# A two-layer hybrid block: operands ahead of a stage border, another order of seven products, and one pass over the context rows

## The chip, the core and the metric

The kernel runs on one core of one Trainium2 chip. The metric is device time in microseconds (us) of one execution. The core has five engines that run side by side, each with its own queue of instructions: TensorE (PE in the profile, its weight loads are PEld), VectorE (DVE), ScalarE (ACT), GpSimd (POOL) and SyncE (SP, which issues nearly all transfers here). TensorE adds up its results in PSUM banks; everything else lives in SBUF tiles.

## The reference

Two layers over 1024 latent tokens and 256 context tokens of width 1024. Each layer mixes tokens (attention, a Fourier transform, a gated mixing), projects, and then runs a squared-ReLU MLP whose result goes through a gate into the residual. The second layer (`last`) updates the latent tokens alone.

```python
def squared_relu_mlp(h, w1, w2):
    return jnp.square(jax.nn.relu(h @ w1)) @ w2

def layer(x, ctx, c, c_ctx, ..., w_out, w1, w2, update_ctx):
    ...
    x = x + gt1 * mix_x
    x = x + gt2 * squared_relu_mlp(modulate(rms_norm(x, g2), sh2, sc2), w1, w2)
    if update_ctx:
        ...
        ctx = ctx + cgt2 * squared_relu_mlp(modulate(rms_norm(ctx, g2), csh2, csc2), w1, w2)
    return x, ctx
```

`w1` is 1024 x 4096, `w2` is 4096 x 1024, all in 32-bit floats.

## The kernel before

**Precision.** Each matrix product is made of three matmuls on operands split into a high and a low part: high x high, high x low, low x high (`mm3`, lines 194 to 196). A split is a cast on ACT (the high part) and a subtraction on DVE (the low part).

**Tokens** come in quads: quad 0 and quad 1 are 512 latent tokens each, quad 2 the 256 context tokens (first layer only).

**First MLP stage** (from line 1641). The 4096 hidden columns are 32 groups of 128, taken in the order p, p+16. For each group and quad, `hidden` makes 24 matmuls, then a ReLU on ACT and a product on DVE into a T tile. After each pair of groups `combine` (line 1485) forms seven left operands from the four hidden tiles of quads 0 and 1 and stores them to DRAM (`tdram[1]` to `tdram[7]`): two as they are, three sums on DVE and two on POOL (line 1494). The context's hidden tiles are stored apart (`put_ctx`, `cdram`).

**Second MLP stage for the latent tokens** (from line 1681). The product with `w2` is done as seven products of half-size blocks instead of eight (Strassen's scheme, `prods`). `turns` is their order. Each product runs over 16 chunks, an item each: `fetch` loads the chunk's left operand (R tiles, two chunks a load) and its block rows of `w2` (blocks 11 and 22 stay in S tiles, with four in L tiles, once loaded; 12 and 21 are loaded into W2 tiles for each use), four items ahead; `split` casts and subtracts the left operand (T tiles, lines 1566 and 1567), sums two weight blocks on POOL where the product needs it (an M tile, line 1573), and splits the sum (W1 tiles, lines 1575 and 1577), two items ahead; `product` makes 4 x 3 matmuls of 512 columns into four PSUM banks. When a product is through, `take` calls wait in the list `todo` and are issued one or two per item: in the first layer they add the gated bank to the residual, in the last to the output tile `z` (its first write is a copy on ACT, line 1613, the others an addition on DVE, line 1615). In the last layer `settle` (line 1617) finishes an output half tile: load of the residual, two POOL operations (lines 1624 and 1625) and, where it is complete, the store. Products 3 and 4 need no sum of weights, the other five need 16 sums each.

The contributions fix when an output block is complete: block (1,1) takes products 4, 1, 5, 7; (2,1) takes 4, 2; (1,2) takes 3, 5; (2,2) takes 3, 1, 2, 6. In the first layer quad 0 is block column 1, and `finish_quad(0)`, the next layer's norm of quad 0 (square sums on ACT and POOL, scaling on DVE, ACT and POOL), starts when it is complete.

**Second MLP stage for the context** (from line 1724, first layer only). The output's 1024 columns are two halves; for each half all 32 chunks are run: `split_ctx` loads 128 rows of `w2`, half the columns (an R tile), and the chunk of context rows (an M tile), and splits both (W1 and T tiles, lines 1730 to 1736), two steps ahead; then 4 x 3 matmuls of 256 columns go into four banks. So the context rows are loaded and split twice.

**What sets the order.** Instructions are written in the order of the program text, but each engine's queue is made by a scheduler that can issue a later instruction earlier when its buffer and operands are there. Tiles of one tag share a fixed number of buffers, and `allocate_in_order` forces them to be taken in program order:

```python
NBUF = {"S": 40, "L": 12, "T": 8, "M": 4, "R": 3, "W1": 8, "W2": 8, "pB": 5}
```

At the border of the two stages the program text has: the last group's hidden tiles (with the loads of items 0 and 1 after its first quad), the last `combine`, the loads of items 2 and 3, then `split(0)` and `split(1)`.

Of the kernel before, what the change touches and what calls it, by code (L numbers as in the profile page):

```python
# [11 lines left out]
F32 = mybir.dt.float32  # L12
# [6 lines left out]
P = 128  # L19
D = 1024  # L20
KC = D // P
# [106 lines left out]
def hybrid_block_kernel(ctx: ExitStack, tc: tile.TileContext, a: dict, out: bass.AP):  # L128
# [45 lines left out]
    def load(dst, src):  # L174
        nc.sync.dma_start(dst, src)
# [420 lines left out]
    def layer(l, ys, norms, bank):  # L596
# [923 lines left out]
        if not last:  # L1520
# [8 lines left out]
                 3: ((11,), None, ((1, 2, 1), (2, 2, 1))), 4: ((22,), None, ((1, 1, 1), (2, 1, 1))),  # L1529
                 5: ((11, 12), ALU.add, ((1, 1, -1), (1, 2, 1))), 6: ((21, 11), ALU.subtract, ((2, 2, 1),)),  # L1530
                 7: ((12, 22), ALU.subtract, ((1, 1, 1),))}
        turns = (4, 3, 1, 5, 7, 2, 6)
        items = [(i, c) for i in turns for c in range(NP)]
        ares, anow, traw, parts_of = {}, {}, {}, {}

# [14 lines left out]
        def fetch(n):  # L1550
            i, c = items[n]
            if c % 2 == 0:
                traw[i, c] = R(2, 512)
                load(flat(traw[i, c]), tdram[i][:, c * 512:(c + 2) * 512])
            for b in prods[i][0]:
                if b in (11, 22):
                    if (b, c) not in ares:
                        ares[b, c] = a_load(b, c)
                else:
                    anow[b, c] = a_load(b, c)  # L1560
# [43 lines left out]
        def take(o, i, j, b, sign):  # L1604
            if not last:
                x, k = xm[j - 1], 4 * (i - 1) + b
                gate = mods[l, 5][:, 0, k:k + 1] if sign > 0 else ngate[:, k:k + 1]
                V.scalar_tensor_tensor(x.chunk(k), o, gate, x.chunk(k), ALU.mult, ALU.add)
                return
            t = out_tile(i, j, b)  # L1610
            if (i, j, b) not in seen:
                seen.add((i, j, b))
                A.copy(t, o)
            else:
                V.tensor_tensor(t, t, o, ALU.add if sign > 0 else ALU.subtract)

# [24 lines left out]
        for n in range(2, NFF):  # L1641
            c = order[n]
            w1c = w1n
            if n + 1 < NFF:
                w1n = split_rows(w1d, order[n + 1], "W1")
            for qi in range(len(quads)):
                hq[c, qi] = hidden(w1c, qi)
                if qi < 2:
                    pump(1)
                if n == NFF - 1 and qi == 0:  # L1650
                    fetch(0)
                    fetch(1)
            if not last:
                put_ctx(c)
            if n % 2:
                combine(c - NP)
        for n in (2, 3):
            fetch(n)
        split(0)
        split(1)  # L1660


        todo = []
# [17 lines left out]
        for n, (i, c) in enumerate(items):  # L1681
            if n + 4 < len(items):
                fetch(n + 4)
            if n + 2 < len(items):
                split(n + 2)
            if c == 0:
                banks = [PB(512) for _ in range(4)]
            tail = last and i == turns[-1]
            if tail and c >= NP - 3:
                if c < NP - 1:  # L1690
                    continue
                assert not todo
                for b in range(4):
                    for cc in range(NP - 3, NP):
                        product(n - NP + 1 + cc, b, banks[b])
                    end_row(banks[b], b)
                continue
            for b in range(4):
                product(n, b, banks[b])
            parts_of.pop(n)  # L1700
            if c > 1 or todo:
                for _ in range(1 if len(todo) < 8 else 2):
                    if todo:
                        todo.pop(0)()
            if side is not None and not todo:
                step(side, 2)
            pump(1)
            if c == NP - 1:
                for b in range(4):
                    for ti, tj, sign in prods[i][2]:  # L1710
                        todo.append(lambda o=banks[b], ti=ti, tj=tj, b=b, sign=sign: take(o, ti, tj, b, sign))
                if last:
                    ready = {5: ((1, 2, True),), 7: ((1, 1, True),), 2: ((2, 1, True), (2, 2, False))}.get(i, ())
                    for b in range(4):
                        for ti, tj, done in ready:
                            todo.append(lambda ti=ti, tj=tj, b=b, done=done: settle(ti, tj, b, done))
                elif i == 2:
                    side = finish_quad(0)
        while todo and last:
            todo.pop(0)()  # L1720
        if not last:
            finish_bg()

            x = xm[2]

            def split_ctx(c, half):
                raw = alloc("R", [512], F32)
                load(raw, w2d[c * P:(c + 1) * P, half * 512:(half + 1) * 512])
                sh, sl = alloc("W1", [512], F32R), alloc("W1", [512], F32R)
                A.copy(sh, raw)  # L1730
                V.tensor_sub(sl, raw, sh)  # L1731
                m = M(256)
                load(m, cdram[:, c * 256:(c + 1) * 256])
                th, tl = pair(T, 256)
                A.copy(th, m)  # L1735
                V.tensor_sub(tl, m, th)  # L1736
                return th, tl, sh, sl

            citems = [(half, c) for half in range(2) for c in range(NFF)]
            ahead = [split_ctx(c, half) for half, c in citems[:2]]  # L1740
            wk, wk_gen = [], None
            for n, (half, c) in enumerate(citems):
                if n + 2 < len(citems):
                    ahead.append(split_ctx(citems[n + 2][1], citems[n + 2][0]))
                if c == 0:
                    banks = [PB(512) for _ in range(4)]
                th, tl, sh, sl = ahead.pop(0)
                for b in range(4):
                    f = slice(b * P, (b + 1) * P)
                    mm3(banks[b][:, 0:256], sh[:, f], sl[:, f], th, tl, c == 0, c == NFF - 1)  # L1750
                if todo:
                    todo.pop(0)()
                elif next(side, 0) == 0 and 1 not in nsum:
                    side = finish_quad(1)
                if half == 1 and c >= 16 and len(wk) < 4 and c % 4 == 0:
                    if wk_gen is None:
                        wk_gen = split_cols(k_pair(("W2", "W1")), a["w_in"][l + 1], 512, 512, L)
                    wk.append(next(wk_gen))
                if c == NFF - 1:
                    for b in range(4):  # L1760
                        k = 4 * half + b
                        V.scalar_tensor_tensor(x.chunk(k), banks[b][:, 0:256], mods[l, 5][:, 1, k:k + 1], x.chunk(k),
                                               ALU.mult, ALU.add)
            run(side)
            run(finish_quad(2))
            return ny, nnorm, (wk, wk_gen)
# [36 lines left out]
```

## Time and profile before

| | |
|---|---|
| median of 3 runs | 2804.55 us (2801.64 to 2808.71) |
| profiled execution | 2804.51 us |
| its span, first to last instruction | 2802.7 us |
| TensorE busy | 2693.4 us, 96% |
| DVE, ACT, POOL busy | 1852.9, 1314.7, 802.4 us |
| mean granted TensorE clock | 0.989 |
| mean DMA rate | 143 GB/s |

Busy time of TensorE overlaps from matmul to matmul, so a busy share of 96% is no measure of its speed; the number of matmuls in a stretch is. A row of the waits or of the timeline names in brackets how long an engine stood idle before an instruction, and what ended that idle time. In the profiled execution the first layer's seven products end at about 1476.7 us and its context pass at about 1592.4; the second layer's products run from 2474.3 to the end.

### The profile page before, as it was taken

Reading aid. Unit: us, or ns where it says so; the run is one execution under the profiler, and the core shown is the slowest. Engines: PE = TensorE matmul, PEld = TensorE weight load, DVE = VectorE, ACT = ScalarE, POOL = GpSimd, SP = SyncE. Lnnn points to the kernel's source line nnn. Section 1 sums busy time; section 2 is a strip of 40 time slices with the busy share of each in tenths; the row PEclk is TensorE's granted clock in tenths of the full one; section 3 lists DMA queues with packets and bytes.
Section 4 is the critical chain, followed back from the end, with each engine's and each line's share of the span. In section 5 each row is a group of like instructions: output and inputs, shape, how many; then the busy total and the mean of one; then the engine's idle time right before and its main releaser. Section 6 shows DMA issues by size and latency. Waiting matters only on the chain.

```text
span 2802.7 us, 39268 instructions
## 1 busy us (share of the span) xinstructions
PE 2693.4 (96%) x13620; PEld 2216.3 (79%) x13620; DVE 1852.9 (66%) x3461; ACT 1314.7 (47%) x2885; POOL 802.4 (29%) x650
## 2 busy tenths in 40 slices
PE   7899898999999999999998999999999999999998
PEld 5677687887888888788878887788888888878876
DVE  7787979767766555465567674888774333354697
ACT  6536878665211111244446534888753222235432
POOL 4221755411011010104451001533211111112587
PEclk9999999999999999999999999999999999999999
DMA  8435221424445454635747723132235333383563
GB/s 281 137 117 153 75 87 47 126 73 158 139 149 182 147 171 149 222 121 166 240 136 219 225 76 121 59 93 70 84 122 190 132 124 128 124 270 98 184 227 115
DMA packets 310919, 401.91 MB, mean 143 GB/s; under 512 B 23336, under 2 KB 201920, under 8 KB 310720
## 3 DMA queue, kind: packets, MB, share of 16 engines
q1 hardware_dynamic: 305568, 390.23, 43.0%
q0 software_dynamic: 5152, 9.18, 1.2%
q8 instruction: 107, 1.75, 0.3%
q14 instruction: 92, 0.75, 0.1%
HBM read 297.87 MB, written 101.45 MB: 142 GB/s over the span
## 4 chain that ended last, share of the span: by engine, by line
PE 63%; DMA 3%; DVE 3%; issue 2%; POOL 2%; ACT 2%; SPq 0%; ACTq 0%; DVEq 0%; POOLq 0%
PE pB L194 19%; PE pB L195 19%; PE pB L196 19%; DMA R<-in_w_mlp 2%; PE pB L1118 2%; PE pB L1131 1%; PE pB L1132 1%; DVE W L1577 1%; PE pB L1039 1%; PE pB L1040 1%; ACT W L1730 0%; DVE T L1567 0%; ACT L L1101 0%; POOL L L1624 0%; PE pB L336 0%
## 5 line engine op out<-in xcount | busy, mean ns | idle before, releaser
L194 PE MATMUL pB<-S,W 128*128 128x512 f32 (+1 forms) x1600 | 599.0, 375 | 2.2 <-ACT S L470 1.6
L196 PE MATMUL pB<-S,W 128*128 128x512 f32 (+1 forms) x1600 | 596.2, 373 | 1.4 <-DVE W L591 1.4
L195 PE MATMUL pB<-S,W 128*128 128x512 f32 (+1 forms) x1600 | 595.4, 373 | 0.3 <-DVE S L475 0.3
L194 PEld LDWEIGHTS pB<-S,W 128*128 128x128 f32 x1600 | 300.7, 188 | 60.3 <-ACT S L470 2.2
L196 PEld LDWEIGHTS pB<-S,W 128*128 128x128 f32 x1600 | 300.7, 188 | 59.2 <-DVE W L591 1.6
L195 PEld LDWEIGHTS pB<-S,W 128*128 128x128 f32 x1600 | 300.9, 188 | 57.8 <-DVE S L475 0.7
L1567 DVE TENSOR_TENSOR T<-R,T 128x512 fp32r<-128x512 f32 x224 | 178.0, 796 | 202.0 <-ACT T L1566 199.5
L1494 POOL TENSOR_TENSOR W<-T,T 128x512 f32<-128x512 f32 x64 | 109.2, 1726 | 704.5 <-issue 600.4
L1468 ACT ACTIVATE M<-pB 128x512 f32<-128x512 f32 (+1 forms) x160 | 88.4, 553 | 463.7 <-PE pB L196 463.7
L1566 ACT CAST T<-R 128x512 fp32r<-128x512 f32 x224 | 139.2, 623 | 305.3 <-PE pB L195 293.0
L195 PE MATMUL pB<-T,W 128*128 128x512 f32 (+1 forms) x704 | 249.4, 356 | 8.1 <-DVE T L1736 4.5
L1121 DVE TENSOR_TENSOR T<-pB,T 128x512 fp32r<-128x512 f32 x328 | 223.4, 686 | 48.7 <-ACT T L1120 44.2
L194 PE MATMUL pB<-T,W 128*128 128x512 f32 (+1 forms) x704 | 244.6, 354 | 8.8 <-ACT T L1735 4.5
L196 PE MATMUL pB<-T,W 128*128 128x512 f32 (+1 forms) x704 | 249.1, 355 | 3.3 <-DVE W L1731 1.9
L1120 ACT CAST T<-pB 128x512 fp32r<-128x512 f32 x328 | 195.2, 600 | 69.5 <-PE pB L1118 33.3
L591 DVE TENSOR_TENSOR W<-R,W 128x512 fp32r<-128x512 f32 x176 | 136.2, 781 | 126.3 <-ACT W L589 126.1
L589 ACT CAST W<-R 128x512 fp32r<-128x512 f32 x192 | 119.1, 623 | 208.9 <-PE pB L195 194.3
L1470 DVE TENSOR_TENSOR T<-pB,M 128x512 f32<-128x512 f32 (+1 forms) x160 | 101.3, 634 | 167.5 <-ACT M L1468 140.3
L1085 DVE TENSOR_REDUCE mb<-pB 128x1 f32<-128x512 f32 x256 | 172.7, 684 | 34.9 <-PE pB L1040 33.6
L194 PE MATMUL pB<-W,T 128*128 128x512 f32 x448 | 176.7, 394 | 5.4 <-ACT W L1575 3.9
L195 PE MATMUL pB<-W,T 128*128 128x512 f32 x448 | 177.3, 396 | 3.3 <-DVE W L1577 3.3
L1101 ACT ACTIVATE L<-pB,nm 128x512 f32<-128x512 f32 x256 | 179.1, 705 | 0.1
(276 smaller groups left out, 5934.2 us busy)
## 6 DMA issues: line engine op xcount, KB each, us to landing
R<-t SPq DMA_DIRECT2D x112, 512.0 KB, 3.9
t<-W SPq DMA_DIRECT2D x160, 256.0 KB, 2.9
R<-in_w_mlp SPq DMA_DIRECT2D x64, 512.0 KB, 4.2
W<-in_w_mlp SPq DMA_DIRECT2D x128, 256.0 KB, 3.1
R<-in_w_ada SPq DMA_DIRECT2D x40, 512.0 KB, 3.8
R<-in_w_out SPq DMA_DIRECT2D x32, 512.0 KB, 4.1
t<-T SPq DMA_DIRECT2D x64, 256.0 KB, 2.6
R<-in_w_mlp SPq DMA_DIRECT2D x64, 256.0 KB, 3.4
```

The source lines that it names most:

```text
L194: E.matmul(o, lh, rh, start=first, stop=False)
L195: E.matmul(o, lh, rl, start=False, stop=False)
L196: E.matmul(o, ll, rh, start=False, stop=last)
L589: A.copy(h, s)
L591: (sub or V).tensor_tensor(lo, s, h, ALU.subtract)
L1085: V.tensor_reduce(ma[:, k + 1:k + 2], tl[k], axis=AX.X, op=ALU.min)
L1101: A.activation(u["pa"][b][:, k * 512:(k + 1) * 512], tl[k], AF.Exp, bias=tl["nm"][:, 0:1], scale=-1.0, accum_out=u["den"][:, b, 1 + k:2 + k])
L1120: A.copy(ph, tp)
L1121: V.tensor_sub(pl, tp, ph)
L1494: (G if n in POOLT else V).tensor_tensor(t, x, y, op)
L1566: A.copy(th, src)
L1567: V.tensor_sub(tl, src, th)
```

## The change

- **Border.** After the first quad of the last hidden group the loads of items 0 to 3 and the splits of items 0 and 1 are issued; before, only the loads of items 0 and 1 stood there. The loads and splits after the loop go.
- **Order of the products.** First layer 4, 2, 1, 5, 7, 3, 6 (before 4, 3, 1, 5, 7, 2, 6); last layer 4, 2, 3, 5, 1, 7, 6. The norm of quad 0 starts after product 7. In the last layer the half tiles (2,1) are settled after product 2, (1,2) after 5, (2,2) in part after 1, (1,1) after 7; before, (1,2) after 5, (1,1) after 7, and (2,1) and (2,2) both after 2. An output tile can now start with a negative product, so its first write is a copy scaled by the sign.
- **Context.** One pass over 32 chunks instead of two. A chunk's context rows and both halves of the weight rows are loaded four chunks ahead into S tiles; both are split two chunks ahead, the weights of odd chunks into L tiles and of even ones into W1 tiles. The eight outputs of 256 columns share four PSUM banks, two to a bank. The eight updates of the residual stand at the end. The four weight splits for the next layer inside the pass come at other chunks (21, 24, 27, 30 of the 32).

```diff
-        turns = (4, 3, 1, 5, 7, 2, 6)
+        turns = (4, 2, 3, 5, 1, 7, 6) if last else (4, 2, 1, 5, 7, 3, 6)
...
-                A.copy(t, o)
+                A.mul(t, o, float(sign))
...
                 if n == NFF - 1 and qi == 0:
-                    fetch(0)
-                    fetch(1)
+                    for m in range(4):
+                        fetch(m)
+                    split(0)
+                    split(1)
...
-        for n in (2, 3):
-            fetch(n)
-        split(0)
-        split(1)
...
-                    ready = {5: ((1, 2, True),), 7: ((1, 1, True),), 2: ((2, 1, True), (2, 2, False))}.get(i, ())
+                    ready = {2: ((2, 1, True),), 5: ((1, 2, True),), 7: ((1, 1, True),),
+                             1: ((2, 2, False),)}.get(i, ())
...
-                elif i == 2:
+                elif i == 7:
                     side = finish_quad(0)
...
-            def split_ctx(c, half):
-                raw = alloc("R", [512], F32)
-                load(raw, w2d[c * P:(c + 1) * P, half * 512:(half + 1) * 512])
-                sh, sl = alloc("W1", [512], F32R), alloc("W1", [512], F32R)
-                A.copy(sh, raw)
-                V.tensor_sub(sl, raw, sh)
-                m = M(256)
+            def fetch_ctx(c):
+                raw = [S(512) for _ in range(2)]
+                for half in range(2):
+                    load(raw[half], w2d[c * P:(c + 1) * P, half * 512:(half + 1) * 512])
+                m = S(256)
                 load(m, cdram[:, c * 256:(c + 1) * 256])
+                return raw, m
+
+            def split_ctx(c, raw, m):
                 th, tl = pair(T, 256)
                 A.copy(th, m)
                 V.tensor_sub(tl, m, th)
-                return th, tl, sh, sl
+                ws = []
+                for half in range(2):
+                    if c % 2:
+                        t = L(2, 512, dt=F32R)
+                        sh, sl = t[:, 0], t[:, 1]
+                    else:
+                        sh, sl = alloc("W1", [512], F32R), alloc("W1", [512], F32R)
+                    A.copy(sh, raw[half])
+                    V.tensor_sub(sl, raw[half], sh)
+                    ws.append((sh, sl))
+                return th, tl, ws
...
+            raws = [fetch_ctx(c) for c in range(4)]
+            ahead = [split_ctx(c, *raws.pop(0)) for c in range(2)]
+            banks = [PB(2, 256) for _ in range(4)]
+            for c in range(NFF):
+                if c + 4 < NFF:
+                    raws.append(fetch_ctx(c + 4))
+                if c + 2 < NFF:
+                    ahead.append(split_ctx(c + 2, *raws.pop(0)))
+                th, tl, ws = ahead.pop(0)
+                for k in range(KC):
+                    sh, sl = ws[k // 4]
+                    f = slice((k % 4) * P, (k % 4 + 1) * P)
+                    o = banks[k // 2][:, k % 2, :]
+                    E.matmul(o, sh[:, f], th, start=(c == 0 and k % 2 == 0), stop=False, skip_group_check=True)
+                    E.matmul(o, sh[:, f], tl, start=False, stop=False, skip_group_check=True)
+                    E.matmul(o, sl[:, f], th, start=False, stop=(c == NFF - 1), skip_group_check=True)
...
+            for k in range(KC):
+                V.scalar_tensor_tensor(x.chunk(k), banks[k // 2][:, k % 2, :], mods[l, 5][:, 1, k:k + 1], x.chunk(k),
+                                       ALU.mult, ALU.add)
```

More of the change, by code (lines that the diff above doesn't have):

```diff
@@ L1736, in split_ctx @@
                 V.tensor_sub(tl, m, th)
-                return th, tl, sh, sl
-            citems = [(half, c) for half in range(2) for c in range(NFF)]
-            ahead = [split_ctx(c, half) for half, c in citems[:2]]
-            wk, wk_gen = [], None
[L1742 to L1750, printed above, removed]
+                ws = []
[11 more added lines that the diff above has]
+            ahead = [split_ctx(c, *raws.pop(0)) for c in range(2)]
+            wk, wk_gen = [], None
+            banks = [PB(2, 256) for _ in range(4)]
[12 more added lines that the diff above has]
+                    E.matmul(o, sl[:, f], th, start=False, stop=(c == NFF - 1), skip_group_check=True)
                 if todo:
@@ L1754, in layer @@
                     side = finish_quad(1)
-                if half == 1 and c >= 16 and len(wk) < 4 and c % 4 == 0:
+                if c >= 20 and len(wk) < 4 and c % 3 == 0:
                     if wk_gen is None:
@@ L1758, in layer @@
                     wk.append(next(wk_gen))
[L1759 to L1763, printed above, removed]
+            for k in range(KC):
+                V.scalar_tensor_tensor(x.chunk(k), banks[k // 2][:, k % 2, :], mods[l, 5][:, 1, k:k + 1], x.chunk(k),
+                                       ALU.mult, ALU.add)
             run(side)
```

## The prediction, made before the run

> **What bounds the kernel now.** I read the busy time by stretches first, then the waits of single stages, then the instructions in order of time around each stage border.
>
> ```profile
> span 2802.7 us, 39268 instructions
> ...
> 1200.00:1300.00 100.00, 100.00 (x443) 82.84 (x442) 59.80 (x94) 41.95 (x74) 24.55 (x19) 1.00 0.37 113
> 1158.60:1170.40 11.80, 6.96 (x19) 5.18 (x18) 9.26 (x10) 4.21 (x8) 5.56 (x4) 0.71 0.53 174
> 2472.70:2484.60 11.90, 7.58 (x24) 5.38 (x24) 10.07 (x10) 4.26 (x8) 7.61 (x5) 0.86 0.79 266
> 1476.70:1592.40 115.70, 102.19 (x769) 95.42 (x770) 78.29 (x141) 65.91 (x142) 14.06 (x12) 0.99 0.75 235
> 2700.00:2743.00 43.00, 41.72 (x180) 33.19 (x179) 43.00 (x34) 17.14 (x30) 37.18 (x24) 1.00 0.67 216
> 2743.00:2798.00 55.00, 49.08 (x195) 37.86 (x194) 43.99 (x48) 14.94 (x26) 42.49 (x27) 0.94 0.29 96
> ...
> 1588.22 0.28 PE L195 MATMUL pB<-T,W 128*128 128x256 f32 x1
> ...
> 1589.66 0.28 PE L195 MATMUL pB<-T,W 128*128 128x256 f32 x1
> ```
>
> After the stretch and its length stand the busy times of PE, PEld, DVE, ACT, POOL with their instructions, the granted clock, DMA share and GB/s. TensorE is the bound: in a quiet part of the second MLP stage it issues 443 matmuls of 512 columns in 100 us, one per 0.226 us. What can be gained is what it loses against that pace:
> - border of the two MLP stages, layer 0: 11.8 us for 19 matmuls (4.3 us): 7.5 lost;
> - the same border, layer 1: 11.9 us for 24 (5.4): 6.5 lost;
> - context pass: 115.7 us for 2 halves x 32 chunks x 12 = 768 matmuls of 256 columns. Twelve of them take 1589.66 - 1588.22 = 1.44 us, 0.12 each, so 92.2 in all: 23.5 lost;
> - the last two products of layer 1: 43.0 - 180 x 0.226 = 2.3 and 55.0 - 195 x 0.226 = 10.9: 13.2 lost (a few missing records make the first too large);
> - the last product of layer 0: its two waits, quoted below, 1.7 us.
> Together 52.4 of 2802.7 us.
>
> **Part 1, the border.** In program order the group's hidden tiles take T buffers (8 of them) before the splits of items 0 and 1 do, and buffers of one tag are taken in that order.
>
> ```profile
> 1142.76 0.62 ACT L1575 CAST W<-L 128x512 fp32r<-128x512 f32 x1 [0.70 <-PE pB L195]
> ...
> 1159.45 1.13 ACT L1566 CAST T<-R 128x512 fp32r<-128x512 f32 x2
> ...
> 1162.96 0.41 DVE L1470 TENSOR_TENSOR T<-pB,M 128x256 f32<-128x256 f32 x1
> ...
> 1160.11 1.20 PE L194 MATMUL pB<-T,W 128*128 128x512 f32 x4 [1.38 <-ACT T L1566]
> 1164.76 0.80 PE L195 MATMUL pB<-T,W 128*128 128x512 f32 x1 [3.46 <-DVE T L1567]
> 1165.35 0.63 PE L196 MATMUL pB<-T,W 128*128 128x512 f32 x1
> 1165.78 0.63 PE L195 MATMUL pB<-T,W 128*128 128x512 f32 x1
> ...
> 2480.34 1.14 ACT L1566 CAST T<-R 128x512 fp32r<-128x512 f32 x2 [5.56 <-POOL W L1494]
> 2480.91 0.65 PE L196 MATMUL pB<-W,T 128*128 128x512 f32 x1 [2.50 <-DVE T L1567]
> ```
>
> The weight casts (L1575) ran as early as 1142.76, so instructions do move ahead where a buffer is free; the T casts (L1566) came only at 1159.45, after the last hidden tile. TensorE waited 1.38 + 3.46 us and then ran at 0.43 us per matmul (1165.35 to 1165.78) instead of 0.226, granted clock 0.71. Layer 1 is alike: 2.50 us, with casts that waited for POOL's combination (L1494). The change gives the four T buffers of items 0 and 1 out before the last hidden tiles. Nothing is added: four casts and four subtractions move under hidden matmuls, where ACT and DVE are mostly idle; the four fetches move ahead of the combination's stores in SP's queue, and their data were stored groups earlier. What is late next: in layer 0 the last hidden tiles now take the 9th and following buffers, so item 2's T waits for the combination or for product item 0. Items 0 and 1 last 24 x 0.226 = 5.4 us, and the combination and one cast and subtraction fit into that by the rows above (1157 to 1163). Bounds: nothing left (gain 14.0), or the whole loss again at item 2 (gain 0). I take 7.0 + 6.0 = 13.0, nearest the rows of the idle ACT, with 0.5 left at each.
>
> A short rest matters by more than its length. The Trainium skill, TensorE: Matmul & The Clock Gate, Part 1, puts the fall to half clock at an idle window of about 3.4 us, so by it each rest of 0.5 us would cost 0.5 us. The trace differs a little: granted clock 0.86 in layer 1's stretch, whose longest single wait is 2.50 us.
>
> **Part 2, the context pass.** Removed: 32 loads of 128 KB, 32 casts and 32 subtractions of 256 columns; the rows of the context come once.
>
> ```profile
> L1730 ACT CAST W<-R 128x512 fp32r<-128x512 f32 x63 | 38.9, 618 | 39.8 <-DMA R<-in_w_mlp 29.3 <-PE pB L195 5.3 <-PE pB L196 3.5
> L1735 ACT CAST T<-M 128x256 fp32r<-128x256 f32 x64 | 24.2, 403 | 6.1 <-DMA M<-tc 6.0
> ...
> L1731 DVE TENSOR_TENSOR W<-R,W 128x512 fp32r<-128x512 f32 x64 | 49.7, 780 | 35.7 <-ACT W L1730 33.9 <-PE pB L196 0.8 <-PE pB L195 0.5
> L1736 DVE TENSOR_TENSOR T<-M,T 128x256 fp32r<-128x256 f32 x64 | 25.8, 427 | 1.7 <-ACT T L1735 1.5
> ...
> L1762 DVE SCALAR_TENSOR_TENSOR L<-pB,mod,L 128x256 f32<-128x256 f32 x4 | 1.7, 476 | 0.0
> L488 POOL TENSOR_TENSOR S<-S,M 128x512 f32<-128x512 f32 x7 | 9.0, 1288 | 15.5 <-ACT M L487 15.4
> ...
> R<-in_w_mlp SPq DMA_DIRECT2D x61, 256.0 KB, 3.4
> M<-tc SPq DMA_DIRECT2D x64, 128.0 KB, 3.3
> ```
>
> ACT saves 12.9 us and DVE 13.7, but neither was full (65.9 and 78.3 of 115.7). What ended last was the load of weight rows: ACT stood 29.3 us for it. Three R buffers, refilled only after a split, face a landing of 3.4 us at 1.44 us per half chunk. The new loop loads four chunks ahead of the product and two ahead of the split into S (40 buffers): 2 x 24 x 0.12 = 5.8 us of lead against 3.4. Per chunk TensorE then needs 2.88 us, ACT 2 x 0.62 + 0.40 = 1.64, DVE 2 x 0.78 + 0.43 = 1.99; the traffic falls by 32 x 0.13 = 4.2 MB from 27 MB, so that in 95 us the rate stays near 240 GB/s and the share near 0.77. The first chunk's operands have no M or R buffer to wait for. S holds 17 tiles of the first quad's norm and at most 15 of these. Eight closing updates stand together now (8 x 0.48 = 3.8 us against 1.9), covered by the next layer's first projections, which read another quad. Bounds: all 23.5 gained, or (waits merely renamed) 0. The rows put DMA, ACT and DVE well under 2.88, so I am near the upper end: 20.5, with 3.0 left for the chunks beside POOL's sums (L488, 1.29 each): the mean of L1731, 0.78 where it lasts 0.68 alone (next row), is 64 x 0.10 = 6.4 us of hindrance in this pass, and the slack of 2.88 - 1.99 a chunk covers about half of it.
>
> ```profile
> 2738.21 0.68 DVE L1567 TENSOR_TENSOR T<-R,T 128x512 fp32r<-128x512 f32 x1
> 2738.81 1.78 DVE L1577 TENSOR_TENSOR W<-M,W 128x512 fp32r<-128x512 f32 x1
> ```
>
> Those 3.0 are the place where a rule speaks against the change: a subtraction of two SBUF tiles lasts 0.68 us alone and 1.78 with POOL at work. At 1.78 throughout, the eight chunks with a sum would cost DVE 2 x 1.78 + 0.43 = 3.99 each, 1.1 over TensorE, 8.9 in all, which is the worst that this row allows. The Trainium skill, SBUF — State Buffer, Who interferes with whom, has one exclusive lock between the two, held for a whole instruction; by it one POOL sum a chunk would delay DVE by 1.29 at most, to 3.3 a chunk, 3.2 us over eight, which no run here shows yet.
>
> **Part 3, the order of the products.** Each product keeps its loads, sums and takes; the blocks of weights are loaded as often as before. The first write of an output tile becomes a scaled copy on ACT, priced as the plain one. What moves is POOL's work in layer 1.
>
> ```profile
> L1573 POOL TENSOR_TENSOR M<-W,S 128x512 f32<-128x512 f32 x10 | 15.8, 1604 | 0.6 <-DVE W L1577 0.6
> L1625 POOL TENSOR_TENSOR L<-L,S 128x512 f32<-128x512 f32 x8 | 12.9, 1617 | 0.5
> L1624 POOL TENSOR_TENSOR L<-L,S 128x512 f32<-128x512 f32 x8 | 12.6, 1580 | 0.0
> ...
> PE pB L194 <- ACT W L1575: 3.9, 2, 3.2
> PE pB L195 <- DVE W L1577: 2.0, 5, 0.6
> ...
> PE pB L196 <- DVE W L1577: 1.2, 1, 1.2
> PE pB L194 <- ACT W L1575: 0.5, 1, 0.5
> ```
>
> In the last product (2745 to 2787) POOL is never idle: 25.5 us settle eight output tiles, and the sums that TensorE needs (L1573) come too late (waits 3.9 + 2.0). Now product 2 is second, its settling falls beside product 3, which needs no sums, and the last product inherits only four tiles of product 7: 12.7 us less. Product 7 with four settlings behind it is what the stretch 2700:2743 shows, at a loss of 2.3. So 13.2 becomes about 3: gain 10 (bounds 13.2 and, if four settlings already choke it, 2). In layer 0 the first quad's norm now runs in product 3, without sums, instead of beside the sums of product 6, which waited 1.2 + 0.5: gain 1.5 (bounds -1 to 1.7; the norm's ACT and DVE work may catch product 3).
>
> **Sum.** 13.0 + 20.5 + 10 + 1.5 = 45 us. The profiled execution took 2804.51 us (span 2802.7 and 1.8 around it), the median of the runs 2804.55, so both give **2759.5**, rounded to 2760.
>
> **Rivals.**
> 1. Splits early, stall one item later: T is short by the four buffers given away, both borders keep their 13. For it: the POOL wait of 5.56 at 2480.34. Against: item 0's own buffers come free after 2.7 us. 2760 + 13 = 2773. Chance 0.10.
> 2. The context pass stays short of operands, by DMA at a share near 0.8 or by DVE beside POOL: half of 23.5 stays, 104 us. 2760 + 9 = 2769; with rival 1, 2782. Chance 0.12.
> 3. The tail stays: four settlings in a burst still starve the sums. 2760 + 8 = 2768. Chance 0.06.
> 4. Slower: two accumulation groups per PSUM bank slow the 256-column matmuls. At 0.19 us instead of 0.12 the pass takes 146 us and eats the other 24.5 and 5.8 more; at the 512-column pace of 0.226 it takes 174 and the kernel 2804.5 + 58 - 24.5 = 2838. Against: nothing in the rows shows a pace by bank. Chance 0.03.
> 5. Nothing lands (waits renamed everywhere): 2804. Chance 0.03.
> My forecast has 0.66. The range reaches down to 2753 (nearly all 52.4 gained) and up to 2783 (rivals 1 and 2 together). A difference under 0.3% (8.4 us) can't be told from no change: faster 0.94, same 0.03, slower 0.03.
>
> **What would show it.** Right: no wait of over 0.5 us on L1566/L1567 at either border and clock 1.00 there; the context pass 93 to 97 us with no ACT wait on weight rows; last product near 46 us with POOL idle between sums; the norm's L470/L488 of the first quad inside product 3. Wrong: a wait on T at item 2 or 3; DVE at 90% or more in the pass; 256-column matmuls over 0.12 us apart; SP held by an output store ahead of a load.

## The result, and the profile after

The changed kernel takes 2763.36 us (median of six runs, 2759.82 to 2768.41), the kernel before 2809.14 us (six runs); the ratio is 0.9842, 95% interval 0.9825 to 0.9859. The profiled execution took 2759.82 us with a span of 2758.1 us, 44.6 us less than the span of before. The prediction was 2760 us.

The stretches of the changed kernel that answer to those of before (start and end, length, then busy time and instructions of PE, PEld, DVE, ACT, POOL, granted clock, DMA share, GB/s):

```profile
1159.10:1170.90 11.80, 11.80 (x56) 9.82 (x55) 8.99 (x14) 5.90 (x11) 2.53 (x3) 1.00 0.86 300
2442.30:2454.20 11.90, 11.87 (x53) 9.48 (x52) 9.69 (x12) 5.92 (x11) 3.44 (x2) 1.00 0.87 299
1470.70:1562.80 92.10, 92.10 (x769) 92.10 (x768) 61.79 (x103) 46.82 (x93) 7.66 (x6) 1.00 0.59 197
2655.00:2698.00 43.00, 41.54 (x179) 32.84 (x177) 43.00 (x38) 17.34 (x30) 36.39 (x24) 1.00 0.53 173
2699.00:2754.00 55.00, 53.19 (x230) 42.39 (x228) 50.58 (x53) 18.30 (x32) 36.50 (x23) 1.00 0.40 132
```

Both borders (first two rows) are full, at clock 1.00. The context pass (third) is full from end to end: 768 matmuls at 0.12 us. Of these stretches only those of the last two products (fourth and fifth; the products run from 2660.9 to 2707.3 us and on to 2753.3) still have gaps. The border of layer 0 in order of time:

```profile
1150.92 1.13 ACT L1566 CAST T<-R 128x512 fp32r<-128x512 f32 x2
...
1158.99 0.28 PE L196 MATMUL pB<-S,W 128*128 128x256 f32 x1
1159.11 0.39 PE L194 MATMUL pB<-T,W 128*128 128x512 f32 x1
...
1161.41 0.62 ACT L1566 CAST T<-R 128x512 fp32r<-128x512 f32 x1 [1.32 <-POOL W L1494]
```

The casts of items 0 and 1 stand 8.2 us ahead of their first matmul, which follows the last hidden one without a gap. Item 2's cast waits for POOL's combination, as foreseen, and nobody waits for it. In the context pass TensorE has no wait at all; the longest waits of ACT are now for TensorE (those for rows of `w2` are 0.8 us in all):

```profile
ACT L L1744 <- PE pB L1766: 15.0, 17, 2.4
...
ACT W L1744 <- PE pB L1765: 11.9, 20, 0.8
```

**A ledger of lost time.** The starts of stages that the change does not touch differ by some us between executions (the last hidden matmul of layer 0 began between 1158.5 and 1167.5 us in the kernels below), so spans alone cannot tell parts of 5 us apart. For each kernel I took the start of every matmul, and summed the distance to the next one less 0.2268 us (512 columns) or 0.12 us (256 columns), the paces of stretches without waits. "First context matmul" is the wait ahead of it.

| us lost | before | whole change | border alone | context alone | order alone | whole, old order in layer 0 |
|---|---|---|---|---|---|---|
| border, layer 0 (30 matmuls) | 7.5 | -0.6 | -0.6 | 6.3 | 3.1 | -0.6 |
| rest of layer 0's products | 1.9 | 3.6 | 1.8 | -0.6 | 5.8 | -0.6 |
| first context matmul | 2.1 | 0.0 | 2.1 | 8.7 | 0.0 | 8.8 |
| context pass | 21.6 | 0.0 | 21.7 | 1.8 | 15.6 | 1.7 |
| border, layer 1 (30 matmuls) | 6.8 | 0.3 | 0.9 | 7.0 | 3.5 | 0.3 |
| rest of layer 1's products | 13.7 | 5.5 | 13.7 | 13.7 | 5.5 | 5.6 |
| sum | 53.6 | 8.8 | 39.6 | 36.9 | 33.5 | 15.2 |
| sum less before | | -44.8 | -14.0 | -16.7 | -20.1 | -38.4 |
| measured, (1 - ratio) x 2807 | | -44.4 | -12.6 | -15.2 | -18.5 | -34.5 |

(The first 30 distances hold a few of 256 columns, hence -0.6.) The three parts alone add to 46.3 us measured, close to the whole, but the rows show that this is not three independent gains: the order alone also shortens both borders and the context pass, and the context part alone gains less than the context pass of the whole shows.

### The profile page after: what moved, and what is told of

Its sections match the earlier page's. It is cut to its first block, busy times and chain, and to the rows that moved or that the text cites. A ratio compares the mean times of both kernels' runs of the same rounds, so it can differ in the third digit from the quotient of the medians.

```text
span 2758.1 us, 39099 instructions
## 1 busy us (share of the span) xinstructions
PE 2679.5 (97%) x13620; PEld 2211.0 (80%) x13620; DVE 1863.3 (68%) x3429; ACT 1301.4 (47%) x2853; POOL 810.6 (29%) x650
## 4 chain that ended last, share of the span: by engine, by line
PE 69%; ACT 2%; DVE 2%; issue 2%; POOL 1%; DMA 1%; SPq 0%; DVEq 0%; POOLq 0%; ACTq 0%
PE pB L194 19%; PE pB L195 19%; PE pB L196 19%; PE pB L1118 2%; PE pB L1765 1%; PE pB L1766 1%; PE pB L1764 1%; PE pB L1131 1%; PE pB L1132 1%; PE pB L1039 1%; PE pB L1040 1%; DVE W L1577 1%; ACT L L1101 0%; PE pB L336 0%; ACT T L1120 0%
## 5 line engine op out<-in xcount | busy, mean ns | idle before, releaser
L1567 DVE TENSOR_TENSOR T<-R,T 128x512 fp32r<-128x512 f32 x224 | 186.5, 834 | 163.8 <-ACT T L1566 163.6
L196 PE MATMUL pB<-T,W 128*128 128x512 f32 x448 | 175.5, 392 | 1.4 <-DVE W L1577 1.1
L194 PE MATMUL pB<-T,W 128*128 128x512 f32 x448 | 174.8, 390 | 0.5 <-ACT W L1575 0.5
L195 PE MATMUL pB<-T,W 128*128 128x512 f32 x448 | 174.5, 389 | 0.0
```

The lines of the kernel that those rows point to most:

```text
L194: E.matmul(o, lh, rh, start=first, stop=False)
L195: E.matmul(o, lh, rl, start=False, stop=False)
L196: E.matmul(o, ll, rh, start=False, stop=last)
L1567: V.tensor_sub(tl, src, th)
```

## Experiments: the three parts alone

**The border part alone** (the kernel before with these two edits):

```diff
-                    fetch(0)
-                    fetch(1)
+                    for m in range(4):
+                        fetch(m)
+                    split(0)
+                    split(1)
...
-        for n in (2, 3):
-            fetch(n)
-        split(0)
-        split(1)
```

> The kernel before with the border part of the change alone: the first operands of the second MLP stage are fetched four at a time and split ahead of the last group of the first stage; the products' order and the two-pass context are those of before. Theory (what held TensorE at the border was the tile buffer's order, the split waiting behind the last group): 13 to 14 us less, 7 us in layer 0 and 6 to 6.5 in layer 1, no wait of TensorE at either border, a ratio near 0.995. Rival (the stall only moves to the third and fourth operands, which are now asked for early and split late): 0 to 3 us less.

Measured: 2793.3 us, ratio 0.9955 [0.9941, 0.9969], 12.6 us less. TensorE has no wait at the border of layer 0 and one of 0.6 us at that of layer 1, at item 2; the losses fall by 8.1 and 5.9 us, and nothing else moves. The rival (the whole stall moves to items 2 and 3) is out.

**Early loads, late splits** (the kernel before with the four fetches early and both splits left where they were):

```diff
-                    fetch(0)
-                    fetch(1)
+                    for m in range(4):
+                        fetch(m)
...
-        for n in (2, 3):
-            fetch(n)
         split(0)
         split(1)
```

> The kernel before with only the fetches of the border part: all four raw operands are asked for in the last group, the splits stay behind it. Theory (the raw operands were there in time, the splits were late because they wait for tile buffers and engines behind the last group): within 2 us of before, and the waits of 2 to 2.5 us at both borders still stand. Rival (the transfers of the operands were late, and asking earlier is what gains): 6 to 13 us less. Third possibility: the four loads displace each other and it is some us slower.

Measured: 2805.51 us, ratio 0.9992 [0.9983, 1.0001], 2.2 us less, with an interval that holds no change too. The losses at the borders are still 6.3 and 5.3 us. So the loads were there in time; the place of the splits in the buffers' order makes the gain.

**The context part alone** (the kernel before with the new `fetch_ctx`, `split_ctx` and the single loop over chunks):

```diff
-            citems = [(half, c) for half in range(2) for c in range(NFF)]
-            ahead = [split_ctx(c, half) for half, c in citems[:2]]
+            raws = [fetch_ctx(c) for c in range(4)]
+            ahead = [split_ctx(c, *raws.pop(0)) for c in range(2)]
...
```

> The kernel before with the context part alone: one pass over 32 chunks with all eight halves of a pair of rows, raw rows and middle rows fetched four chunks ahead, two accumulators in one bank. Theory: the context pass falls from 115.6 us to 92 us, 768 matmuls at 0.12 us each, so about 23 us less, a ratio near 0.992, and nothing else moves. Rival (half of the stall comes with the transfers and stays): 9 to 12 us less. Rival (two accumulators in one bank cost time, and the gain comes from elsewhere in the change): above 2800 us.

Measured: 2791.41 us, ratio 0.9946 [0.9933, 0.9959], 15.2 us less, between the theory and the first rival. The pass itself takes 94.0 us, but ahead of it TensorE now waits (timeline of this kernel; here the context's T cast is L1736):

```profile
1482.85 1.01 PE L1765 MATMUL pB<-T,W 128*128 128x256 f32 x3 [8.49 <-ACT T L1736]
```

8.5 us for the first split, where the kernel before waited 2 us. The wait is the context part's together with the old order, as the next runs show. The rival with two accumulators in one bank is out: the matmuls stand 0.12 us apart.

**The order alone** (the kernel before with the new turns, the sign in the first taking, and the settlings and the norm behind their products):

```diff
-        turns = (4, 3, 1, 5, 7, 2, 6)
+        turns = (4, 2, 3, 5, 1, 7, 6) if last else (4, 2, 1, 5, 7, 3, 6)
...
-                A.copy(t, o)
+                A.mul(t, o, float(sign))
...
-                elif i == 2:
+                elif i == 7:
                     side = finish_quad(0)
```

> The kernel before with the order of the seven products alone (and the sign in the first taking of a quadrant, the settlings and the norm that go with it). Theory: layer 1's end loses about 8 us, because fewer settlings fall on the last two products; layer 0's products change by less than 1 us; in all 7 to 9 us less, a ratio near 0.997. Rival (the end is bound by the last taking and the output's transfers, whatever the order): within 2 us of before.

Measured: 2789.85 us, ratio 0.9934 [0.9921, 0.9948], 18.5 us less: twice what I expected. By the ledger layer 1's products give 8.2, as expected. The rest lies where I had put nothing: the borders give 4.4 and 3.3, the context pass with its first wait 8.1, and layer 0's products take 3.9 back.

The gain at the borders shows in the order of time. First the kernel before, then the order alone:

```profile
1159.60 3.44 DVE L1577 TENSOR_TENSOR W<-L,W 128x512 fp32r<-128x512 f32 x2
...
1160.78 3.38 POOL L1573 TENSOR_TENSOR M<-S,L 128x512 f32<-128x512 f32 x2
```

```profile
1163.43 2.37 DVE L1577 TENSOR_TENSOR W<-L,W 128x512 fp32r<-128x512 f32 x2
...
1166.78 0.50 PE L195 MATMUL pB<-T,W 128*128 128x512 f32 x1 [1.65 <-DVE T L1567]
...
1174.35 1.30 POOL L1573 TENSOR_TENSOR M<-W,L 128x512 f32<-128x512 f32 x1 [9.71 <-DMA W<-in_w_mlp]
```

In the kernel before POOL had sums to do at the border, far ahead of use: product 1, third in the order, sums two blocks that are resident. With product 2 second, the first sums wait for the transfer of another block and come after the border. DVE's two subtractions then last 2.37 us in place of 3.44, TensorE's wait is 1.65 in place of 3.46 us, and the clock does not fall (below). This link is read from the rows; no run takes these sums alone away from the border.

## Experiments: what the context pass waited for

**Layer 0's order put back** (the whole change, but):

```diff
-        turns = (4, 2, 3, 5, 1, 7, 6) if last else (4, 2, 1, 5, 7, 3, 6)
+        turns = (4, 2, 3, 5, 1, 7, 6) if last else (4, 3, 1, 5, 7, 2, 6)
...
-                elif i == 7:
+                elif i == 2:
```

> The whole change, with layer 0's order of products as it was before (4, 3, 1, 5, 7, 2, 6) and its norm behind the sixth of them. Theory, from the trace of the whole change, where layer 0's last products still wait 1.6 us against 1.7 before: the order gains nothing in layer 0, so this is within 1.5 us of the whole change. The prediction's step would have it 1.5 us slower than the whole change. Rival (the new order even costs 1 us there): 1 to 2 us faster than the whole change.

Measured: 2770.66 us, ratio 0.9877 [0.9863, 0.989]; against the whole change (2763.36) 7.3 us more. All three expectations fail. The ledger's last column says where: the products themselves get better by 4.2 us (3.6 to -0.6), but the first context matmul waits 8.8 us and the pass loses 1.7. The chain of work that ended last, in order of time (start, duration, what):

```profile
1470.18 0.74 DVE M L468
1470.92 1.33 DVE L L1608 x2
...
1472.26 0.34 SPq L178
...
1473.95 4.55 DMA S<-tc
...
1478.52 0.41 ACT T L1735
...
1478.98 1.01 PE pB L1764 x3
```

L468 is a step of the first quad's norm on DVE, L1608 are two takings that stand behind it, and L178 is the store of a residual tile, which waits for the second taking. SP issues the first loads of the context pass straight behind this store. The context rows land at 1478.50 us, and the cast for which TensorE waits (8.60 us) begins at 1478.52. So the norm holds back the loads, and through them the first split (by then ACT and POOL hold nothing up). In the whole change the norm starts one product earlier, the same loads leave 35 to 47 us ahead of the pass, and the cast comes 4 us ahead of it:

```profile
1423.57 0.43 SPq L175 DMA_DIRECT2D S<-in_w_mlp  x1
...
1435.48 0.42 SPq L175 DMA_DIRECT2D S<-tc  x1
...
1466.56 0.40 ACT L1735 CAST T<-S 128x256 fp32r<-128x256 f32 x1
```

Why SP has these loads so late is argued, not shown: they take S tiles, which are given out in program order behind those of the norm. The norm's last S tile (L473) is begun at 1423.1 us in the whole change, just ahead of the first load at 1423.57, and at 1474.3 here, 1.6 us behind the first load at 1472.65 (the order binds the scheduler, not the engines).

So layer 0's order is worth 6.4 us by the ledger, 7.3 by the medians and 9.9 by the ratios, and all of it falls due at the start of the context pass.

**Two passes, deep loads** (the kernel before with its two passes and old order; raw rows in S tiles, asked for seven items ahead):

```diff
-                raw = alloc("R", [512], F32)
+                raw = S(512)
...
-                m = M(256)
+                m = S(256)
...
+            raws = [fetch_ctx(c, half) for half, c in citems[:7]]
...
+                if n + 7 < len(citems):
+                    raws.append(fetch_ctx(citems[n + 7][1], citems[n + 7][0]))
```

> The kernel before with its two context passes kept, but with raw rows and middle rows in the large pool and asked for seven items ahead in place of two. Nothing else differs. Theory (the pass lost 23 us because its loads were asked for only two items, some 3 us, ahead, and land in about that time): most of the loss goes, the pass falls from 115.6 us to 92 to 98 us, and the kernel takes 18 to 23 us less than before. Rival (the pass lost it because each item's three splits, the middle rows' done twice, hold ScalarE and VectorE, and the single pass saves half of the middle rows' splits): 0 to 8 us less.

Measured: 2799.87 us, ratio 0.998 [0.997, 0.999], 5.6 us less. The total lies in the rival's range, but the pass, 97.4 us, in the theory's: it lost 5.2 us in place of 21.6, so lead time takes away 16 us of its loss. Half of this is lost again: the first wait grew from 2.1 to 7.5 us and layer 0's products from 1.9 to 4.9 (waits of this kernel, 1455 to 1570 us; the profiled execution, 2804.28 us, was the slowest of twelve):

```profile
PE pB L194 <- ACT T L1738: 7.3, 1, 7.3
PE pB L195 <- DVE T L1739: 2.4, 3, 1.4
```

Here too the first load of the pass leaves straight behind a store that waited for a taking (at 1490.09 us, 6 us ahead of the first matmul). Seven items of depth do not help when the first load is late. POOL's norm adds about 1 us: the first rows had landed by 1494.07, and ACT, waiting for POOL, casts them from 1495.14.

**New order, two passes, deep loads** (the edits of the run before this one and of the order alone, on the kernel before):

```diff
-        turns = (4, 3, 1, 5, 7, 2, 6)
+        turns = (4, 2, 3, 5, 1, 7, 6) if last else (4, 2, 1, 5, 7, 3, 6)
...
-                raw = alloc("R", [512], F32)
+                raw = S(512)
...
+            raws = [fetch_ctx(c, half) for half, c in citems[:7]]
```

> The kernel before with the new order of products and, in its two context passes, the deep fetches (raw rows seven items ahead in the large pool); the border is that of before and the rows of the context still come twice. Theory (two causes stand behind the context pass's loss: the first quad's norm beside the last product of layer 0, which holds back the first splits, and loads asked for too late; the number of passes is no cause): the pass falls to 92 to 95 us as with one pass, some 13 us less than with the order alone, so 2774 to 2779 us. Rival (loading and splitting the context rows twice costs something that only one pass takes away): the pass stays at 98 us or more, 2782 us or more.

Measured: 2785.23 us, ratio 0.9926 [0.9913, 0.9938]. The pass takes 99.3 us. The theory missed by 6 us or more; the rival's figures hold. Of the miss, some 2.6 us lie in layer 0's products, which lose 8.4 us in place of the 5.8 of the order alone. For the pass the rows qualify the rival (stretches and TensorE's waits):

```profile
1483.00:1500.00 17.00, 12.44 (x84) 11.62 (x84) 16.91 (x25) 10.11 (x24) 10.78 (x7) 0.90 0.86 281
1500.00:1582.00 82.00, 82.00 (x685) 82.00 (x684) 58.94 (x113) 52.63 (x114) 2.82 (x3) 1.00 0.69 225
```

```profile
PE pB L196 <- DVE W L1737: 4.2, 3, 1.8
```

After its first 17 us the pass with double loads and splits loses nothing: 685 matmuls in 82.00 us. All 7.1 us are lost at the start, where DVE is full (16.91 of 17.00) beside POOL at work. One pass asks for fewer splits per matmul there (three for 24 matmuls, where two passes need four); that this is why it has no such start is argued, not shown.

**One pass, shallow loads** (the whole change, with rows in R and M tiles, fetched only where they are split):

```diff
-                raw = [S(512) for _ in range(2)]
+                raw = [alloc("R", [512], F32) for _ in range(2)]
...
-            raws = [fetch_ctx(c) for c in range(4)]
-            ahead = [split_ctx(c, *raws.pop(0)) for c in range(2)]
+            ahead = [split_ctx(c, *fetch_ctx(c)) for c in range(2)]
```

> The whole change, but in the single context pass the raw rows and middle rows use the pools of before and are asked for only where they are split, two chunks ahead (a chunk is 2.9 us of matmuls, so some 5.8 us ahead). Theory (lead time is what counts): a chunk is twice as long as an item of before, so two chunks give twice the lead, but the splits stand right behind their loads on ScalarE and VectorE: half or more of the 23 us is lost again, 2773 to 2787 us. Rival (it was the number of splits and passes): the time of the whole change, 2763 us, within 2 us.

Measured: 2776.73 us, ratio 0.9898 [0.9883, 0.9913], 13 us more than the whole change, in the theory's range. The pass loses 6.6 us; another 6.7 lie behind it, in the first 200 matmuls of the next layer (51.2 us in place of 44.5; waits from 1565 to 1610 us):

```profile
PE pB L194 <- ACT W L552: 2.9, 2, 2.5
PE pB L195 <- DVE W L553: 0.9, 2, 0.7
```

The splits of the next layer's first weights come late too. Lead time, with the larger pool that it needs, is worth 13 us even in the single pass.

## Experiments: the end of layer 1

**Late settlings** (the whole change; the third quadrant's settlings behind product 7):

```diff
-                    ready = {2: ((2, 1, True),), 5: ((1, 2, True),), 7: ((1, 1, True),),
+                    ready = {5: ((1, 2, True),), 7: ((1, 1, True), (2, 1, True)),
```

> The whole change, with layer 1's settlings of the third quadrant put behind product 7 with the fourth quadrant's, so that eight settlings lie in the last two products in place of four. The order of the products is the new one. Theory (the tail lost its time because the takings queue behind the settlings on VectorE and GpSimd, and the banks come free late): most of the 8 us of the tail comes back, 6 to 8 us slower than the whole change, with TensorE's waits on VectorE's takings in the last products. Rival (the order itself, with its takings per product, makes the tail short): within 2 us of the whole change.

Measured: 2766.99 us, ratio 0.9866 [0.9853, 0.988], 3.6 us more than the whole change, between the theory and the rival. Layer 1's products lose 10.3 us in place of 5.5, and TensorE's waits on the low parts grow from the first row (whole change, 2640 to 2757 us) to the second (this run, 2640 to 2764):

```profile
PE pB L195 <- DVE W L1577: 2.8, 8, 0.4
```

```profile
PE pB L195 <- DVE W L1577: 6.5, 13, 1.6
```

But the edit did not bring about what it was meant to. Each of the last two products has four settlings, as in the whole change: the scheduler left the multiplications of the third quadrant beside product 3, and moved three of its four additions to product 1. The extra loss lies in products 1 and 7 (2.5 and 5.8 us in place of 0.3 and 2.8); the last product loses 2.1 us, no more than the 2.5 of the whole change. So the run shows that POOL's settlings cost time beside sums, and not what eight of them in the end would cost.

**Settlings one per three items, and takings one per two items.** Two runs on the whole change; the second has both edits:

```diff
-                            todo.append(lambda ti=ti, tj=tj, b=b, done=done: settle(ti, tj, b, done))
+                            lag.append(lambda ti=ti, tj=tj, b=b, done=done: settle(ti, tj, b, done))
...
+            if not todo and lag and c % 3 == 0:
+                lag.pop(0)()
```

```diff
-                for _ in range(1 if len(todo) < 8 else 2):
+                few = not last and i == turns[-1]
+                for _ in range(c % 2 if few else 1 if len(todo) < 8 else 2):
```

> The whole change, with layer 1's settlings issued one per three items in place of a burst of four. Theory (the 5.5 us that layer 1's products still lose come from the takings and the sums behind a burst of settlings on GpSimd, with VectorE slowed beside it): 2 to 4 us less than the whole change, about 2760 us. Rival (the number of settlings beside a product counts, not their bunching): within 1 us of the whole change.

> The whole change, with the settlings of layer 1 spread as in the kernel run before this one, and in layer 0's last product the eight takings of the product before issued one per two items in place of one per item. Theory (layer 0 still loses 3.5 us in the first third of its last product, where VectorE is busy 93% with takings beside the splits of sums): 1.5 to 3 us less than with the settlings spread alone, some 2757 us. Rival (the sums on GpSimd set the pace there, the takings don't): no change. Third possibility (the late takings hold the banks that the context pass needs): 1 to 3 us more.

Measured: 2764.84 us, ratio 0.9858 [0.9844, 0.9871], and 2765.96 us, ratio 0.9859 [0.9844, 0.9874]. Neither tells anything of bunching: in both traces DVE, ACT and POOL run the same instructions in the same order as in the whole change. Only ten of SP's transfers stand elsewhere. What these runs give is, nearly, two more measurements of the whole change: the three medians differ by up to 2.6 us, so the 3.6 us of late settlings rest on the ledger.

**Settlings on VectorE** (the whole change, but):

```diff
-            G.tensor_tensor(zt, zt, grow2[i - 1], ALU.mult)
-            G.tensor_tensor(zt, zt, x, ALU.add)
+            V.tensor_tensor(zt, zt, grow2[i - 1], ALU.mult)
+            V.tensor_tensor(zt, zt, x, ALU.add)
```

> The whole change, with the two operations of each settling in layer 1 on VectorE in place of GpSimd. Theory (in the last two products VectorE is full because its subtractions last 1.78 us beside GpSimd's work and 0.68 us alone: sixteen settling operations on GpSimd cost VectorE up to 16 x 1.1 = 17.6 us there, and would cost it 16 x 0.68 = 10.9 us as its own): the 5.5 us that layer 1's products still lose fall to 1 to 4 us, the kernel takes 1 to 4 us less than the whole change. Rival (VectorE is busy all the time there, and sixteen more operations make it later): 2 to 8 us more, with longer waits of TensorE on VectorE's low parts (L1577).

Measured: 2757.38 us (2755.18 to 2758.73), ratio 0.9814 [0.98, 0.9827]: faster than both kernels, some 6 us under the whole change (2758.73 at most here, 2759.82 at least there). Layer 1's products now lose nothing (-0.2 in place of 5.5 us), and no wait of TensorE is left from 2640 us on. Stretches of the whole change, then of this kernel:

```profile
2640.00:2700.00 60.00, 58.54 (x252) 46.63 (x251) 60.00 (x53) 24.25 (x43) 48.99 (x31) 1.00 0.52 169
2700.00:2757.00 57.00, 52.19 (x225) 41.55 (x224) 50.54 (x54) 17.40 (x31) 36.13 (x22) 1.00 0.39 128
```

```profile
2640.00:2700.00 60.00, 60.00 (x267) 49.67 (x265) 58.14 (x63) 25.29 (x46) 34.84 (x24) 1.00 0.58 183
2700.00:2757.00 57.00, 51.16 (x226) 42.04 (x224) 44.73 (x60) 17.57 (x31) 19.79 (x13) 0.98 0.37 120
```

DVE takes over POOL's work and is *less* busy: 58.14 + 44.73 = 102.9 us, with 123 instructions, in place of 60.00 + 50.54 = 110.5 with 107. The groups of instructions from 2600 us on say why (busy time, mean ns; whole change first):

```profile
L1577 DVE TENSOR_TENSOR W<-M,W 128x512 fp32r<-128x512 f32 x51 | 80.9, 1585 | 0.0
L1567 DVE TENSOR_TENSOR T<-R,T 128x512 fp32r<-128x512 f32 x51 | 50.9, 998 | 8.5 <-ACT T L1566 8.5
```

```profile
L1577 DVE TENSOR_TENSOR W<-M,W 128x512 fp32r<-128x512 f32 x53 | 53.6, 1012 | 0.0
L1567 DVE TENSOR_TENSOR T<-R,T 128x512 fp32r<-128x512 f32 x52 | 43.9, 845 | 14.9 <-ACT T L1566 14.5
L1624 DVE TENSOR_TENSOR L<-L,S 128x512 f32<-128x512 f32 x12 | 13.2, 1134 | 0.0
...
L1625 DVE TENSOR_TENSOR L<-L,S 128x512 f32<-128x512 f32 x12 | 12.2, 1037 | 0.0
```

The subtractions cost 131.8 us beside POOL's settlings and 97.5 without them, 34.3 less; the settlings add 25.4. The Trainium skill, SBUF — State Buffer, Who interferes with whom, has an exclusive lock between the two engines; these means agree with it.

The last product alone shows the trend over four kernels: with eight settlings on POOL (before) it lost 10.9 us, with four 2.5 (order alone and whole change), with none 0. Between the first and the others the takings on DVE change too, from eight to four.

## Why the prediction was right, and where it was not

The total was right: 45 us predicted, 44.6 in the profile, 44.4 in the runs. That it is right to within 1 us is luck, for single terms were off by up to 3.2 us and the errors cancel. Its terms, by the ledger:

- **Border, 7.0 + 6.0.** Measured 8.1 + 6.5 (part alone: 8.1 + 5.9). The mechanism is shown by two runs (splits early: all gained; loads early: 2 us). Of the two rests of 0.5 us left for item 2, little came in the whole change (0.3 us in layer 1).
- **Context pass, 20.5.** The whole change took 21.6 in the pass and 2.1 ahead of it, 23.7; but the part alone gained 15.2. "What ended last was the load of weight rows" holds, and for the start of the pass as well. The step that failed is "The first chunk's operands have no M or R buffer to wait for", as if they could then be there in time: with the old order their loads left behind the norm (8.5 us of waiting in the part alone, 8.6 with layer 0's order put back). The prediction's last sign of being wrong, an output store ahead of a load, is just what these two runs show. The 3.0 us left for DVE beside POOL's sums did not appear; splits ran two chunks ahead and DVE was busy 61.79 of 92.10 us.
- **Layer 0's norm, 1.5 (bounds -1 to 1.7).** The worst-sized term. I priced the norm's new place by the two waits inside the product (1.7 us). Those did not go: the rest of the products lost 1.7 *more*; DVE is busy 23.23 of 25 us at the start of product 6. What the norm's place decides is the start of the context pass, and undoing it cost 10.5 us there, 6.4 net. I had credited that gain to the deeper loads alone, so the two errors cancel: 20.5 + 1.5 = 22.0 predicted, 23.7 - 1.7 = 22.0 found.
- **Tail, 10 (about 3 left).** Measured 8.2, with 5.5 left. The last product takes 46.0 us in place of 54.5, as the prediction's sign had it, and the waits on casts behind POOL's late sums (L1575, 3.9 us) are gone. Short by a term: the settlings that stay also slow DVE's subtractions beside them, in the last product (2.5 us) and in product 7 (2.8). Moving the settlings to DVE removed all 5.5.
- **Not foreseen:** the order alone shortens both borders by 7.7 us, by the rows through POOL's sums, which no longer lie there. In the whole change this is hidden, since the border part takes the same loss.
- **Rivals.** 1 (stall moves on) and 4 (two groups in a bank) are out. 2 (pass stays short of operands) is out for the whole, but with shallow loads it comes true, at 6.6 us. 3 (tail stays) came true in part, 2 of its 8 us. 5 is out.

## What to carry to other kernels

When a stage starts late, follow the loads of its *first* tile back to where they are issued, and see what stands ahead of them in the queue and in the order of their buffers: here a norm placed one product too late held them back, cost 6 to 10 us, and showed as the next stage's loss. Asking for more tiles ahead does not help when the first load is late. Parts tested alone may add up to the right sum by accident; test at least one part by taking it out of the whole as well. An engine that is full with subtractions may become less busy by taking work over from GpSimd. And where a scheduler reorders the instructions, look in the trace for what an edit moved before reading its time.

## What the runs showed of the hardware

**The clock fell in stretches of 3.41 us or twice that, and not by the length of a wait.** In the recorded clock of the kernel before and of the run with early loads every stretch at half clock within these stages lasted 3.41 or 6.83 us. With early loads and late splits, layer 1's border had these waits:

```profile
2475.03 0.50 PE L194 MATMUL pB<-W,T 128*128 128x512 f32 x1 [1.47 <-ACT T L1566]
...
2476.63 1.15 PE L196 MATMUL pB<-W,T 128*128 128x512 f32 x2 [0.41 <-DVE T L1567]
2477.58 0.63 PE L194 MATMUL pB<-W,T 128*128 128x512 f32 x1
2478.01 0.63 PE L195 MATMUL pB<-W,T 128*128 128x512 f32 x1
```

1.47 + 0.41 us of rest, and then matmuls 0.43 us apart, half pace. With the order alone, layer 0's border rested 1.38 + 1.65 us, and its clock stayed at 1.00:

```profile
1162.40:1174.20 11.80, 8.77 (x40) 6.86 (x39) 9.01 (x14) 5.35 (x10) 2.24 (x2) 1.00 0.77 262
```

So a larger rest may pass and a smaller one not. The Trainium skill, TensorE: Matmul & The Clock Gate, Part 1, has a free-running window of 3413 ns; the lengths of the half-clock stretches agree with it, and rests split over two windows would explain the second case, which no run here isolates. The prediction's reading of that page, by which short rests cost only their own length, does not hold here: 1.9 us in two pieces were enough. In the recorded clock of the whole change there is no half-clock stretch from 495.7 us to the end of its span.

**VectorE and GpSimd.** Moving the settlings from GpSimd to VectorE gained 5.7 us in the products. By the groups above, 24 such operations took 25.4 us of VectorE as its own, 1.06 each, and had cost it 34.3 us, 1.43 each, on GpSimd, by what they added to the subtractions beside them. The Trainium skill, Perfetto Trace Analysis, Optimizing Scalar/DVE Operations, has it that moving operations between these two "might not help"; in this case, and in this direction, it helped.
